# Attention masks of a hybrid decoder block: one mask product of 256 columns per bank instead of one of 128 per diagonal block

## The chip, the core and the metric

The kernel runs on one core of a Trainium2 chip. A core has TensorE for matrix products (PE in the rows, its weight loads PEld), VectorE (DVE), ScalarE (ACT), GpSimd (POOL), and SyncE (SP), which here issues every DMA. The metric is device time in microseconds (us). Before the change it is 869.69 us, the median of three runs from 869.67 to 869.99 us.

## The reference, cut to what matters

The program is one decoder block on 512 tokens of width 1024: RMS norm, a combined input projection, stick-breaking attention and an RWKV-7 branch, a gated merge, a squared-ReLU MLP, a gated embedding and a last norm. The change touches the attention alone, which has 8 heads of 64 channels:

```python
z = jnp.einsum('bhqd,bhkd->bhqk', q[:, :, q0:kend], k[:, :, :kend]).astype(jnp.float32) * scale
mask = s_pos < t_pos
log_om = jnp.where(mask, jax.nn.log_sigmoid(-z), 0.0)
rev = lax.cumsum(log_om, axis=log_om.ndim - 1, reverse=True)
log_w = jax.nn.log_sigmoid(z) + rev - log_om
w = jnp.where(mask, jnp.exp(log_w), 0.0)
```

The mask is strictly causal: a query sees the keys before it. In blocks of 128 keys by 128 queries only the four diagonal blocks need it; blocks under the diagonal are never computed.

## The kernel before, in words

Float32 products are made of pieces in fp32r: a value is split into a high and a low part, and a product of the input projection is three matmuls of 512 columns (lines 191 to 193, high times high, high times low, low times high). Eight such triples make one projected tile of 128 features by 512 tokens, in a PSUM tile `ps_m` or `ps_z`. The split of a loaded weight tile `w_raw` is one ScalarE cast (`w_hi`, line 175) and one VectorE subtraction (`w_lo`, line 176).

Attention works per head, with keys on the partitions and queries along the columns. Of the 4 key blocks j, block j meets the queries from 128 j on, so it has 512, 384, 256 or 128 columns (`ZN`). The scores lie in three PSUM banks: block 2 in one (256 columns), blocks 1 and 3 together in one (384 + 128), block 0 in one (512). `scores` fills the banks in that order. For each block it issues a product with the high part of q (line 458), one with its low part (line 459), and a mask product (line 460): the bf16 identity as weights times `caus_b`, a 128 x 128 tile that holds -1e30 where key >= query and 0 elsewhere, so that the mask is added to the diagonal block in PSUM. That makes 4 masks per head and 32 in all. Per bank follow Abs, Exp and Ln on ScalarE (lines 463 to 465), a VectorE step that gives the softplus `sp` (line 466), and its split into `sph` and `spl` (line 222).

`attend` then adds, into the same banks, the sums over later keys (products with `tri` and `neg`, lines 505 and 509), takes the exponential (ScalarE, line 510), splits it into `wh` and `wl` (VectorE, lines 511 and 512), and multiplies by the values into `ps_o` (line 497). `projected` makes q and k of a pair of heads ready: `qT`, `kT` and `vT` are scaled out of PSUM by VectorE (lines 394, 406, 414), the high parts are cast by ScalarE (400, 409) and GpSimd (401), the low parts `ql` and `kk` come from VectorE (402, 410). Four transposes (line 421) turn the values.

`drive` interleaves the steps of three generators in the source: the attention of one head, the scores of the next, and projection products that fill TensorE's time. The order in which each engine then runs the instructions isn't the order of the source alone: a scheduler places them by its own estimates of their lengths, so a change in a few instructions can move others. Each engine runs its list in order and waits at the first instruction whose operands aren't there.

Of the kernel before, what the change touches and what calls it, by code (L numbers as in the profile page):

```python
# [12 lines left out]
BF16 = mybir.dt.bfloat16  # L13
# [5 lines left out]
P = 128  # L19
# [31 lines left out]
K_ID, K_ONE, K_STRICT, K_INCL, K_B8, K_O8, K_S8, K_BO8, K_BO, K_TRI, K_NEG, K_CAUS = range(12)  # L51
# [34 lines left out]
def tile_block(ctx: ExitStack, tc: tile.TileContext, xT, xt, pT, wts, lora, cols_d, gfin_d, consts_d, out, dbg=None):  # L86
    nc = tc.nc
    act, dve, pool, pe, sync = nc.scalar, nc.vector, nc.gpsimd, nc.tensor, nc.sync
# [3 lines left out]
    def r32(ap):  # L92
        return ap.bitcast(F32)
# [126 lines left out]
    def split(hi, lo, src):  # L220
        act.copy(out=hi, in_=src)  # L221
        dve.tensor_tensor(out=lo, in0=src, in1=r32(hi), op=ALU.subtract)
# [37 lines left out]
    def rstd_of(pool_, ps, ssum, r=None):  # L260

        n = ssum.shape[-1]
        pe.matmul(ps, onesd, ssum, start=True, stop=True)
        if r is None:
            r = pool_.tile([P, T], F32, name="rstd", bufs=2)[:, 0:n]
        nt = pool_.tile([P, T], F32, name="nt", bufs=1)[:, 0:n]
        state["square"] = rsqrt(r, nt, ps)
        return r
# [8 lines left out]
    with ExitStack() as sA:  # L277
# [43 lines left out]
        with ExitStack() as s1:  # L321
            p1 = s1.enter_context(tc.tile_pool(name="p1", bufs=2))
            ps1 = s1.enter_context(tc.tile_pool(name="ps1", bufs=2, space=PSUM))

            def ps_z():
                return ps1.tile([P, T], F32, name="ps_z", bufs=5)

            ZB = [0, 512, 1024, 896]
            ZN = [512, 384, 256, 128]
            BANKS = [(0, 512), (512, 512), (1024, 256)]  # L330

# [44 lines left out]
            first = p1.tile([P, 4 * P], F32, name="first", tag="sums", bufs=1)  # L376
            sync.dma_start(out=first, in_=consts_d[:, NCONST:NCONST + 4 * P])
            tri, neg = (p1.tile([P, P], F32R, name=n, bufs=1) for n in ("tri", "neg"))
            ident_b, caus_b = (p1.tile([P, P], BF16, name=n, bufs=1) for n in ("ident_b", "caus_b"))

            def c1(k):
                return first[:, COFF[k] - NCONST:COFF[k] - NCONST + P]
# [55 lines left out]
            def z(zt, j, lo=0, n=None):  # L438

                b = 0 if j == 0 else (2 if j == 2 else 1)  # L440
                s = ZB[j] - BANKS[b][0] + lo
                n = ZN[j] - lo if n is None else n
                return zt[b][:, s:s + n]

            def scores(hp, hh, got):

                qq, ql, kk = heads[hp][:3]
                sp = p1.tile([P, 1280], F32, name="sp")
                sph = p1.tile([P, 1280], F32R, name="sph")
                spl = p1.tile([P, 1280], F32R, name="spl")  # L450
                zt = {}
                got.update(zt=zt, sp=sp, sph=sph, spl=spl)
                for b, js in BLOCKS:
                    zt[b] = ps_z()

                    for j in js:
                        s = slice(j * P, (j + 1) * P)
                        pe.matmul(z(zt, j), kk[hh][:, s], qq[hh][:, j * P:T], start=j < 3, stop=False, skip_group_check=True)
                        pe.matmul(z(zt, j), kk[hh][:, s], ql[hh][:, j * P:T], start=False, stop=False, skip_group_check=True)
                        pe.matmul(z(zt, j, 0, P), ident_b, caus_b, start=False, stop=True, skip_group_check=True)  # L460
                    s, n = BANKS[b]
                    e = sp[:, s:s + n]
                    act.activation(out=e, in_=zt[b][:, :n], func=AF.Abs)
                    act.activation(out=e, in_=e, func=AF.Exp, scale=-1.0)
                    act.activation(out=e, in_=e, func=AF.Ln, bias=1.0)
                    dve.scalar_tensor_tensor(out=e, in0=zt[b][:, :n], scalar=0.0, in1=e, op0=ALU.max, op1=ALU.add)
                    split(sph[:, s:s + n], spl[:, s:s + n], e)
                    if b == 1:

                        sums = p1.tile([P, 512], F32, name="sums", bufs=1)  # L470
                        hi, lo = (p1.tile([P, 640], F32R, name=name) for name in ("sums_hi", "sums_lo"))
                        for to, i in ((0, 2), (256, 1)):
                            for part, d in ((sph, hi), (spl, lo)):
                                pool.tensor_copy(out=d[:, to:to + P], in_=part[:, ZB[i]:ZB[i] + P])
                        dve.tensor_tensor(out=sums[:, 0:P], in0=sp[:, ZB[2] + P:ZB[2] + 2 * P], in1=sp[:, ZB[3]:ZB[3] + P], op=ALU.add)
                        split(hi[:, P:2 * P], lo[:, P:2 * P], sums[:, 0:P])
                        for c, other in ((0, sp[:, ZB[2]:ZB[2] + P]), (P, sums[:, 0:P])):
                            dve.tensor_tensor(out=sums[:, 256 + c:384 + c], in0=sp[:, ZB[1] + P + c:ZB[1] + 2 * P + c], in1=other, op=ALU.add)
                        pool.tensor_copy(out=hi[:, 384:640], in_=sums[:, 256:512])
                        pool.tensor_tensor(out=lo[:, 384:640], in0=sums[:, 256:512], in1=r32(hi[:, 384:640]), op=ALU.subtract)  # L480
                        got["later"] = hi, lo
                    yield

            def attend(hp, hh, got):
# [8 lines left out]
                def output(js):  # L493

                    for j in js:
                        for part in (wh, wl):
                            pe.matmul(ps_o[:, j * P:T], vv[:, j, hh, :, :].rearrange("p a d -> p (a d)"),  # L497
                                      part[:, ZB[j]:ZB[j] + ZN[j]], start=j == 2 and part is wh, stop=j == 0 and part is wl,
                                      skip_group_check=True)
# [32 lines left out]
            for _ in islice(v, 1):  # L532
# [4 lines left out]
            dve.tensor_copy(out=ident_b, in_=ident)  # L537
            dve.tensor_scalar(out=omm, in0=cols[:, COLS["mu"]:COLS["mu"] + 14], scalar1=-1.0, scalar2=1.0,
                              op0=ALU.mult, op1=ALU.add)
            dve.tensor_copy(out=caus_b, in_=c1(K_CAUS))  # L540
            rstd_of(p1, ps_z(), ssum, rs)
            for i in range(2):
                projected(0, i, pss[i])
# [21 lines left out]
            ahead = with_late(early())  # L565
            NSTEP = 11
            drive((3, scores(*heads_[0], parts[heads_[0]])), (NSTEP, islice(ahead, NSTEP)))
            for n, g in enumerate(heads_):
                todo = [(5, attend(*g, parts[g])), (NSTEP, islice(ahead, NSTEP))]
                if n + 1 < len(heads_):  # L570
                    todo.insert(1, (3, scores(*heads_[n + 1], parts[heads_[n + 1]])))
                drive(*todo)
# [4 lines left out]
        with ExitStack() as s2:  # L577
# [37 lines left out]
            for hp in range(HP):  # L615
                csl = slice(hp * P, (hp + 1) * P)
                for i, (name, got) in enumerate((("w0", cum_), ("a0", a_all))):
# [3 lines left out]
                    t = p2.tile([P, T], F32, name=name, bufs=HP)  # L621
# [497 lines left out]
    def kept(tt):  # L1119
        t = p4.tile([P, 512], F32, name="pl", tag="rk", bufs=4)  # L1120
        return t

    for half in range(2):
        for tt in (half * 2, half * 2 + 1):
            t = kept(tt)
# [222 lines left out]
    with tc.issue_after(s_):  # L1348
        act.preload_act_table_set(LNEXP)

        r, n = (r4[:, i, tt:tt + 1] for i in (1, 2))
# [74 lines left out]
```

## Time and profile before

| what | value |
|---|---|
| median of 3 runs | 869.69 us |
| the profiled execution's own time | 869.75 us |
| its span, first to last instruction | 867.7 us |
| TensorE matmul busy | 851.4 us, 98% of the span |
| VectorE busy | 678.1 us, 78% |
| ScalarE busy | 448.6 us, 52% |
| mask products (line 460) | 32, from 33.0 to 126.9 us |

A row of the timeline gives start, duration, engine, line, operation, and output <- inputs. Matmuls are pipelined: the duration of a short one reaches into those after it, so what a matmul takes from TensorE is read from start to start. A bracket at the end of a row is the idle time before it, and what ended it.

### The profile page before, as it was taken

Reading aid. Unit: us, or ns where it says so; the run is one execution under the profiler, and the core shown is the slowest. Engines: PE = TensorE matmul, PEld = TensorE weight load, DVE = VectorE, ACT = ScalarE, POOL = GpSimd, SP = SyncE. Lnnn points to the kernel's source line nnn. Section 1 sums busy time; section 2 is a strip of 40 time slices with the busy share of each in tenths; the row PEclk is TensorE's granted clock in tenths of the full one; section 3 lists DMA queues with packets and bytes.
Section 4 is the critical chain, followed back from the end, with each engine's and each line's share of the span. In section 5 each row is a group of like instructions: output and inputs, shape, how many; then the busy total and the mean of one; then the engine's idle time right before and its main releaser. Section 6 shows DMA issues by size and latency. Waiting matters only on the chain.

```text
span 867.7 us, 13424 instructions
## 1 busy us (share of the span) xinstructions
PE 851.4 (98%) x5182; PEld 686.8 (79%) x5182; DVE 678.1 (78%) x1228; ACT 448.6 (52%) x703; POOL 80.4 (9%) x138
## 2 busy tenths in 40 slices
PE   8999999999999999999999999999999999999996
PEld 5778787877777777777888888888888888888885
DVE  7899987896979888776754789858985987697767
ACT  6888887744335343534424464344434543453744
POOL 1432431002302111020000000000000000000000
PEclk9999999999999999999999999999999999999999
DMA  7212212221121224437935621531252034300422
GB/s 269 98 49 66 82 62 85 74 97 51 62 87 57 80 73 153 141 116 258 318 121 181 232 73 38 182 120 49 83 184 98 25 127 164 98 1 0 170 73 98
DMA packets 32272, 95.32 MB, mean 110 GB/s; under 512 B 3664, under 2 KB 3664, under 8 KB 32208
## 3 DMA queue, kind: packets, MB, share of 16 engines
q1 hardware_dynamic: 32208, 94.46, 32.6%
q8 instruction: 41, 0.67, 0.3%
q14 instruction: 23, 0.19, 0.1%
HBM read 83.96 MB, written 10.49 MB: 109 GB/s over the span
## 4 chain that ended last, share of the span: by engine, by line
PE 81%; DVE 10%; ACT 4%; issue 1%; DMA 1%; SPq 0%; POOL 0%; POOLq 0%; DVEq 0%; ACTq 0%
PE ps_m L191 13%; PE ps_m L193 13%; PE ps_m L192 13%; PE ps_m L206 9%; PE ps_m L207 9%; PE ps_m L208 9%; DVE w_lo L176 2%; PE ps_g L817 1%; PE ps_o L497 1%; PE ps_g L193 1%; PE ps_c L935 1%; PE ps_s L944 1%; PE ps_g L191 1%; PE ps_g L192 1%; PE ps_g L906 1%
## 5 line engine op out<-in xcount | busy, mean ns | idle before, releaser
L175 ACT CAST w_hi<-w_raw 128x1024 fp32r<-128x1024 f32 x94 | 99.0, 1053 | 170.4 <-PE ps_m L192 110.8
L176 DVE TENSOR_TENSOR w_lo<-w_raw,w_hi 128x1024 fp32r<-128x1024 f32 x94 | 115.1, 1225 | 37.6 <-ACT w_hi L175 37.2
L191 PE MATMUL ps_m<-h_hi,w_hi 128*128 128x512 f32 x320 | 130.6, 410 | 0.9 <-ACT h_hi L353 0.9
L192 PE MATMUL ps_m<-h_lo,w_hi 128*128 128x512 f32 x320 | 128.0, 400 | 0.0
L193 PE MATMUL ps_m<-h_hi,w_lo 128*128 128x512 f32 x320 | 127.5, 399 | 0.0
L191 PE MATMUL ps_m<-hx,w_hi 128*128 128x512 f32 x256 | 99.6, 390 | 0.4 <-ACT hx L1049 0.4
L192 PE MATMUL ps_m<-hx,w_hi 128*128 128x512 f32 x256 | 99.6, 390 | 0.0
L193 PE MATMUL ps_m<-hx,w_lo 128*128 128x512 f32 x256 | 99.5, 389 | 0.0
L191 PEld LDWEIGHTS ps_m<-h_hi,w_hi 128*128 128x128 f32 x320 | 60.7, 190 | 11.4 <-ACT h_hi L353 1.6
L193 PEld LDWEIGHTS ps_m<-h_hi,w_lo 128*128 128x128 f32 x320 | 60.3, 188 | 11.8
L192 PEld LDWEIGHTS ps_m<-h_lo,w_hi 128*128 128x128 f32 x320 | 60.5, 189 | 11.0 <-DVE h_lo L354 1.1
L191 PEld LDWEIGHTS ps_m<-hx,w_hi 128*128 128x128 f32 x256 | 48.0, 188 | 10.5 <-ACT hx L1049 0.6
L192 PEld LDWEIGHTS ps_m<-hx,w_hi 128*128 128x128 f32 x256 | 48.1, 188 | 10.2 <-DVE hx L1050 0.2
L193 PEld LDWEIGHTS ps_m<-hx,w_lo 128*128 128x128 f32 x256 | 48.0, 188 | 10.0
L207 PE MATMUL ps_m<-w_lo,fS 128*128 128x512 f32 x128 | 49.8, 389 | 0.0
L208 PE MATMUL ps_m<-w_hi,fS 128*128 128x512 f32 x128 | 49.8, 389 | 0.0
L206 PE MATMUL ps_m<-w_hi,fS 128*128 128x512 f32 x128 | 49.8, 389 | 0.0
L1291 POOL TENSOR_SCALAR r<-s 128x1 f32<-128x1 f32 x1 | 0.5, 519 | 478.9 <-DVE t L1271 478.9
L208 PE MATMUL ps_m<-w_hi,fA 128*128 128x512 f32 x96 | 37.4, 389 | 0.0
L207 PE MATMUL ps_m<-w_lo,fA 128*128 128x512 f32 x96 | 37.3, 389 | 0.0
L206 PE MATMUL ps_m<-w_hi,fA 128*128 128x512 f32 x96 | 37.3, 389 | 0.0
L221 ACT CAST fS<-sums 128x256 fp32r<-128x256 f32 (+1 forms) x32 | 19.8, 620 | 33.3 <-DVE sums L1141 33.3
(378 smaller groups left out, 1911.6 us busy)
## 6 DMA issues: line engine op xcount, KB each, us to landing
w_raw<-in_wts_dram SPq DMA_DIRECT2D x98, 512.0 KB, 3.5
gates<-gg SPq DMA_DIRECT2D x16, 256.0 KB, 2.1
x_in<-in_xT_dram SPq DMA_DIRECT2D x8, 256.0 KB, 5.7
tmp<-gates SPq DMA_DIRECT2D x8, 256.0 KB, 4.0
upsb<-tmp SPq DMA_DIRECT2D x8, 256.0 KB, 3.5
ga<-upsb SPq DMA_DIRECT2D x8, 256.0 KB, 5.4
gb<-gates SPq DMA_DIRECT2D x8, 256.0 KB, 5.4
xs<-in_xt_dram SPq DMA_DIRECT2D x4, 512.0 KB, 5.9
```

Source lines behind the costliest of these rows:

```text
L175: act.copy(out=hi, in_=raw)
L176: dve.tensor_tensor(out=lo, in0=raw, in1=r32(hi), op=ALU.subtract)
L191: pe.matmul(ps, wh, xh[:, k, t], start=first, stop=False)
L192: pe.matmul(ps, wh, xl[:, k, t], start=False, stop=False)
L193: pe.matmul(ps, wl, xh[:, k, t], start=False, stop=last)
L206: pe.matmul(ps, xh[:, k + j], wh, start=first and j == 0, stop=False, skip_group_check=True)
L207: pe.matmul(ps, xh[:, k + j], wl, start=False, stop=False, skip_group_check=True)
L208: pe.matmul(ps, xl[:, k + j], wh, start=False, stop=last and j == 1, skip_group_check=True)
L221: act.copy(out=hi, in_=src)
L497: pe.matmul(ps_o[:, j * P:T], vv[:, j, hh, :, :].rearrange("p a d -> p (a d)"), part[:, ZB[j]:ZB[j] + ZN[j]], start=j == 2 and part is wh, ...
L817: last = pe.matmul(ps[rows, k], left[rows, k, :], rhs[rows, k], start=True, stop=True)
L906: pe.matmul(ps[:, j * P:(j + 1) * P], Z[:, hh * 4 + g * 2 + cp, :], MA[:, g * 4 + j, :], start=True, stop=True)
```

## The change

Three things change in the attention, and one around it.

1. In the bank of blocks 1 and 3, block 3 now comes first (columns 0 to 127 of the bank) and block 1 behind it (128 to 511), so that both diagonal blocks lie side by side. The table `ZB` says so, and all later steps take their columns from it.
2. `caus_b` grows from one 128 x 128 tile to three side by side: the mask, the mask again, zeros. The zeros are written once by GpSimd, the two masks by one VectorE cast of 256 columns.
3. The mask product moves out of the loop over blocks: one per bank, of 256 columns. For blocks 1 and 3 it takes mask and mask; for a bank with one block it takes mask and zeros. That makes 3 per head and 24 in all, each of 256 columns.
4. The reserved scratch for DMA descriptors written by software shrinks to 2048 bytes per partition, which makes room for the wider tile; every SBUF address moves down by 14,336 or 13,824 bytes.

```diff
-            ZB = [0, 512, 1024, 896]
+            ZB = [0, 640, 1024, 512]
...
-            ident_b, caus_b = (p1.tile([P, P], BF16, name=n, bufs=1) for n in ("ident_b", "caus_b"))
+            ident_b = p1.tile([P, P], BF16, name="ident_b", bufs=1)
+            caus_b = p1.tile([P, 3, P], BF16, name="caus_b", bufs=1)
+            pool.memset(caus_b[:, 2], 0.0)
...
                         pe.matmul(z(zt, j), kk[hh][:, s], ql[hh][:, j * P:T], start=False, stop=False, skip_group_check=True)
-                        pe.matmul(z(zt, j, 0, P), ident_b, caus_b, start=False, stop=True, skip_group_check=True)
+
+                    pe.matmul(z(zt, js[-1], 0, 2 * P), ident_b, caus_b[:, 0:2] if len(js) == 2 else caus_b[:, 1:3], start=False, stop=True,
+                              skip_group_check=True)
...
-            dve.tensor_copy(out=caus_b, in_=c1(K_CAUS))
+            dve.tensor_copy(out=caus_b[:, 0:2], in_=c1(K_CAUS).rearrange("p (o t) -> p o t", o=1).broadcast_to([P, 2, P]))
...
-    nc = bacc.Bacc("TRN2", target_bir_lowering=False, num_devices=1)
+    nc = bacc.Bacc("TRN2", target_bir_lowering=False, num_devices=1, dynamic_dma_scratch_size=2048)
```

From the scores of the fifth of the eight heads on, the lists of all engines are the same as before except for the masks. Up to there the scheduler places other instructions differently too. The line numbers below 376 stay; after it they grow by 2, and after line 460 by 4.

TensorE, first head, bank of blocks 1 and 3 of the scores, before:

```order
L458 MATMUL ps_z<-qq_271,kk_281 128x384
L459 MATMUL ps_z<-ql_193,kk_281 128x384
L460 LDWEIGHTS ident_b
L460 MATMUL ps_z<-caus_b,ident_b 128x128
L458 MATMUL ps_z<-qq_271,kk_281 128x128
L459 MATMUL ps_z<-ql_193,kk_281 128x128
L460 LDWEIGHTS ident_b
L460 MATMUL ps_z<-caus_b,ident_b 128x128
L192 MATMUL ps_m<-h_lo,w_hi 128x512
```

TensorE, the same place after the change, with what now comes behind it:

```order
L460 MATMUL ps_z<-qq_272,kk_282 128x384
L461 MATMUL ps_z<-ql_194,kk_282 128x384
L460 MATMUL ps_z<-qq_272,kk_282 128x128
L461 MATMUL ps_z<-ql_194,kk_282 128x128
L463 LDWEIGHTS ident_b
L463 MATMUL ps_z<-caus_b,ident_b 128x256
L193 MATMUL ps_z<-h_hi,w_lo 128x512
L191 MATMUL ps_z<-h_hi,w_hi 128x512
L192 MATMUL ps_z<-h_lo,w_hi 128x512
L193 MATMUL ps_z<-h_hi,w_lo 128x512
L191 MATMUL ps_m<-h_hi,w_hi 128x512
```

The mask between the two blocks is gone and the one behind them is wider. In this first head the scores also come five projection matmuls earlier: the four of `ps_z` and the first of `ps_m` that stood ahead of them now stand behind. The four transposes, likewise, moved ahead by five matmuls (not shown).

VectorE, the first pair of heads, from `rs` (the norm's factors) on, before and after as one difference:

```order
L257 SCALAR_TENSOR_TENSOR rs<-nt,rs 128x512
-L176 TENSOR_TENSOR w_lo<-w_raw,w_hi 128x1024
-L394 SCALAR_TENSOR_TENSOR qT<-ps_m,rs 128x512
-L406 TENSOR_TENSOR kT<-ps_m,rs 128x512
-L414 TENSOR_TENSOR vT<-ps_z,rs 128x512
+L396 SCALAR_TENSOR_TENSOR qT<-ps_m,rs 128x512
+L408 TENSOR_TENSOR kT<-ps_m,rs 128x512
+L416 TENSOR_TENSOR vT<-ps_z,rs 128x512
```

The weight split `w_lo` that stood ahead of `qT` is gone from here; after the change it stands behind the `kk` of both heads.

VectorE, the third head's attention and the fourth head's first scores, before:

```order
L511 CAST wh<-sp 128x256
L512 TENSOR_TENSOR wl<-sp,wh 128x256
L511 CAST wh<-sp 128x512
L466 SCALAR_TENSOR_TENSOR sp<-ps_z,sp 128x256
L512 TENSOR_TENSOR wl<-sp,wh 128x512
```

VectorE, the same place after the change:

```order
L515 CAST wh<-sp 128x256
L470 SCALAR_TENSOR_TENSOR sp<-ps_z,sp 128x256
L516 TENSOR_TENSOR wl<-sp,wh 128x256
L515 CAST wh<-sp 128x512
L222 TENSOR_TENSOR spl<-sp,sph 128x256
L516 TENSOR_TENSOR wl<-sp,wh 128x512
```

The softplus `sp` of the fourth head's first bank has moved ahead of the third head's `wl`.

## Rows read from the trace of the kernel before

**Rows 1.** The page: the chain that ended last, by engine.
```profile
PE 81%; DVE 10%; ACT 4%; issue 1%; DMA 1%; SPq 0%; POOL 0%; POOLq 0%; DVEq 0%; ACTq 0%
```
**Rows 2.** Windows: stretch, length, PE, PEld, DVE, ACT, POOL busy (instructions), clock, DMA share, GB/s.
```profile
30.00:50.00 20.00, 19.11 (x95) 14.15 (x95) 19.41 (x37) 18.61 (x37) 8.44 (x12) 1.00 0.23 77
50.00:140.00 90.00, 89.11 (x457) 72.90 (x457) 80.65 (x148) 74.02 (x136) 27.17 (x43) 1.00 0.18 62
```
**Rows 3.** Line 460: the mask matmuls, ns min/median/max, first and last start.
```profile
L460 PE MATMUL ps_z<-caus_b,ident_b x32: 229/230/232, 33.0 to 126.9; 128*128 128x128 bf16 x32
```
**Rows 4.** Timeline of PE, bank of blocks 1 and 3: start, us, engine, instruction.
```profile
69.85 0.33 PE L459 MATMUL ps_z<-ql,kk 128*128 128x384 f32 x1
70.03 0.23 PE L460 MATMUL ps_z<-caus_b,ident_b 128*128 128x128 bf16 x1
...
70.32 0.23 PE L460 MATMUL ps_z<-caus_b,ident_b 128*128 128x128 bf16 x1
70.36 0.48 PE L191 MATMUL ps_m<-h_hi,w_hi 128*128 128x512 f32 x1
70.68 0.39 PE L192 MATMUL ps_m<-h_lo,w_hi 128*128 128x512 f32 x1
```
**Rows 5.** Timeline of PE: a matmul of 256 columns and its successors.
```profile
92.74 0.28 PE L509 MATMUL ps_z<-sums_lo,neg 128*128 128x256 f32 x1
92.86 0.40 PE L191 MATMUL ps_m<-h_hi,w_hi 128*128 128x512 f32 x1
93.09 0.40 PE L192 MATMUL ps_m<-h_lo,w_hi 128*128 128x512 f32 x1
```
**Rows 6.** Timeline of DVE: the mask's cast, and the next wait.
```profile
20.74 0.22 DVE L540 CAST caus_b<-first 128x128 bf16<-128x128 f32 x1
...
24.13 1.23 DVE L176 TENSOR_TENSOR w_lo<-w_raw,w_hi 128x1024 fp32r<-128x1024 f32 x1 [2.04 <-ACT w_hi L175]
```
**Rows 7.** Timeline of POOL: its first cast after the memsets.
```profile
29.24 1.28 POOL L401 CAST qq<-qT 64x512 fp32r<-64x512 f32 x2 [25.74 <-DVE qT L394]
```
**Rows 8.** Timeline of PE at the first transposes and the first scores.
```profile
29.69 0.39 PE L191 MATMUL ps_z<-h_hi,w_hi 128*128 128x512 f32 x1
30.43 0.66 PE L421 MATMUL ps_m<-cst,vT 128*128 128x128 f32 x4 [0.35 <-DVE vT L414]
...
32.65 0.36 PE L458 MATMUL ps_z<-qq,kk 128*128 128x256 f32 x1 [0.17 <-DVE kk L410]
```
**Rows 9.** Timeline of DVE from the norm's factors to the low part of k.
```profile
25.99 0.69 DVE L257 SCALAR_TENSOR_TENSOR rs<-nt,rs 128x512 f32<-128x512 f32 x1
27.35 1.23 DVE L176 TENSOR_TENSOR w_lo<-w_raw,w_hi 128x1024 fp32r<-128x1024 f32 x1 [0.67 <-ACT w_hi L175]
28.49 0.68 DVE L394 SCALAR_TENSOR_TENSOR qT<-ps_m,rs 128x512 f32<-128x512 f32 x1
...
31.81 1.41 DVE L410 TENSOR_TENSOR kk<-kT,kk 64x512 fp32r<-64x512 f32 x2
```
**Rows 10.** Timeline of PE in and at the end of the first head's attention.
```profile
38.21 0.47 PE L191 MATMUL ps_m<-h_hi,w_hi 128*128 128x512 f32 x1
38.78 0.33 PE L509 MATMUL ps_z<-sph,neg 128*128 128x128 f32 x1
...
48.60 0.50 PE L497 MATMUL ps_o<-wh,vv 128*128 128x512 f32 x1
...
49.49 0.50 PE L497 MATMUL ps_o<-wl,vv 128*128 128x512 f32 x1 [0.16 <-DVE wl L512]
```
**Rows 11.** Timelines at 68 us: DVE, ACT and PE around the third head's first `wl`.
```profile
68.16 0.42 DVE L512 TENSOR_TENSOR wl<-sp,wh 128x256 fp32r<-128x256 f32 x1
...
68.31 0.41 ACT L465 ACTIVATE sp<-sp 128x256 f32<-128x256 f32 x1
...
68.63 0.39 PE L497 MATMUL ps_o<-wl,vv 128*128 128x256 f32 x1
```
**Rows 12.** Timeline of PE after the long VectorE chain from 82 to 95 us.
```profile
95.63 0.39 PE L497 MATMUL ps_o<-wl,vv 128*128 128x256 f32 x1 [0.55 <-DVE wl L512]
```

## The prediction

> **What bounds the kernel now.** I read the chain of waits first: TensorE carries 81% of it, VectorE 10% [rows 1]. The windows over the attention then show two stretches that differ. From 50 to 140 us TensorE is busy in 89.11 of 90 us; from 30 to 50 us TensorE and VectorE are level, 19.11 and 19.41 of 20 us [rows 2]. So what TensorE no longer does is worth its time after 50 us, and before that only as far as VectorE is earlier too. Third, the starts on TensorE's timeline, since the 0.23 us that a mask is said to last [rows 3] reaches into its successors. From 140 us on nothing is changed in any list, and I let what is won or lost by then pass to the end unchanged.
>
> **What a mask costs.** Behind a mask of 128 columns the next matmul starts 0.04 us later, but that next one then takes 0.32 us to its successor, where the same kind of matmul, not behind a mask, takes 0.23 [rows 4, 5]. A mask therefore costs 0.04 + 0.09 = 0.13 us, though its 128 columns, at the 0.23 us of 512, are worth 0.058. A matmul of 256 columns takes 0.12 us and leaves its successor at the normal 0.23 [rows 5]. I read this as a floor: the next weights need about 0.12 us to load, a matmul of 256 columns covers that and one of 128 doesn't. If so, a mask of 256 columns costs what one of 128 costs.
>
> *The 24 masks that stay, 128 to 256 columns.* By rows 5 the change is 0.12 - 0.13, nothing or a gain of 0.01 each, 0.24 us in all. The other bound is that 128 more columns come on top, 0.058 each, 24 x 0.058 = +1.4 us. I take 0, since a row shows a matmul of that width with just such a successor; that it is fp32r and the mask bf16 is the part that no row shows.
>
> [...]
>
> *The 8 masks that go,* one per head, between the score products of blocks 1 and 3: 8 x 0.13 = 1.0 us of TensorE. If the weight load is left uncovered all the same by the 128-column score product behind it, only the 0.04 is saved, 0.3 us in all. I take 0.13, since the two masks of rows 4 stand in one group of four short matmuls that takes 0.83 us from 69.85 to 70.68, less 0.17 and 0.23 for the long ones at its ends: 0.43 us, or 0.11 per short matmul, whichever kind. Of the eight, two fall before 50 us and are counted below. One, at 82 us, falls into a stretch in which VectorE is the later one: TensorE idles 0.55 us for `wl` at 95.63 [rows 12], at the end of an unbroken run of VectorE work that starts at about 82 us, so that mask only lengthens the idle time. Five remain: 5 x 0.13 = -0.65 us.
>
> **What the moved instructions do at the start.** Before, `rs` is there at 25.99 + 0.69 = 26.7 us, but VectorE first waits 0.67 us for a weight cast and runs `w_lo`, so that `qT` starts at 28.49 [rows 9]. With that `w_lo` moved behind `kk`, `qT` can start at 26.7, `kT` and `vT` behind it. The low parts need ScalarE's casts, and ScalarE is done with its own `w_hi` at about 27.3, so `kk` of the first head moves from 31.81 + 0.7 to about 30.6. The transposes stood at 30.43, though the matmul ahead of them, started at 29.69, leaves TensorE free at 29.92: 0.51 us lost [rows 8]. Five matmuls earlier they would be reached at 29.92 - 5 x 0.23 = 28.8, and `vT` ends at about 28.5: no wait. The first scores are reached 0.41 us (four transposes) and six matmuls (1.4 us) later, at 30.6, when `kk` comes: no wait, or a tenth, where before 0.17 us was idle [rows 8]. So TensorE wins up to 0.7 us here. The moved `w_lo` is for a product that TensorE reaches after 40 us; its weight buffer is refilled some 4 us later, SP's next load being queued for that buffer, and those weights are first cast at about 42 us, so 4 us fit in.
>
> Up to 50 us the total then goes by VectorE, busy in nearly all of it: what it wins is the 0.67 us that it idled ahead of `w_lo`, and a few tenths of later waits. TensorE's waits at 48.60 and 49.49 are for `wh` and `wl` [rows 10]. VectorE now does two more sums of 0.2 us ahead of that `wh`, but TensorE has three more matmuls ahead of that `wl`. I take -0.9 us at 50 us, two masks included. Bounds: -1.6, if all of TensorE's waits that I found in the stretch go: 0.51 and 0.17 from above, 0.25 at 38.78 (0.57 from the start before it, of which 0.32 is a matmul behind a mask), 0.43 from 48.60 to 49.49 (0.89 for two matmuls of 0.23), and two masks, 0.26 [rows 8, 10]; and +0.9 on the other side, worked out with the third rival.
>
> **What they do at 68 us.** `wl` now stands behind the `sp` of the next head's first bank. Before, TensorE started its product with `wl` at 68.63, right behind `wl`'s 68.16 + 0.42 [rows 11]. `sp` needs ScalarE's Ln (line 465), which ended at 68.31 + 0.41; its list changed too, so that the Ln comes ahead of a 512-column exponential and ends at about 68.3. Then `sp` takes 0.34, `wl` follows from 68.65 on and ends near 69.07: TensorE waits 0.47 us more. Behind `wl` stand two `wh` and a split, which TensorE needs only at 72 us. Bounds: 0, if VectorE is ahead of TensorE by then, and 0.5. I take +0.47.
>
> **What is hidden.** The cast of `caus_b` grows from 0.22 us by at most that much and stands ahead of a VectorE wait of 2.04 us [rows 6]; GpSimd's memset lies in a wait of 25.74 us [rows 7]. Without that cover they would cost 0.22 us and the length of a small memset. The smaller scratch changes addresses only; no DMA here is issued by GpSimd.
>
> **The sum.** -0.65 - 0.9 + 0.47 = -1.08 us, on the profiled execution's 869.75 (867.7 of span and 2.05 around it), which is 0.06 above the median: 868.7, or 868.6 against the median. Its own range is 867.6 to 869.4.
>
> **Rivals.**
> First, more is won at the start: all these waits go, -1.6, the one at 68 us doesn't come, and the five masks give -0.65: -2.25, or 867.5 (between 866.8 and 867.9). For it: nearly all of them are for VectorE, whose list lost an idle stretch. Against it: VectorE is busy 97% of that stretch, so it can hardly be 1.6 us earlier.
>
> Second, a mask costs by its columns: 24 x 0.115 - 32 x 0.058 = +0.9 us, of which about 0.8 lies where TensorE is the later one. With the start without its masks (-0.64) and +0.47: +0.6, or 870.3. For it: bf16 and fp32r needn't behave alike. Against it: 0.13 us per mask in the trace before, more than twice its columns. [...]
>
> Third, the other side: the early scores stop TensorE. They stand five projection matmuls earlier in its list, and if `kk` isn't earlier (the point is 31.5 us: `kk` later than that costs more than the waits that go), TensorE stands still with five matmuls behind them, 5 x 0.23 = 1.16 us, that were done by then before. +1.16 - 0.26 - 0.65 + 0.47 = +0.7, or 870.4; with the columns' price on top 871.3. For it: VectorE's `kk` waits on ScalarE, which is as busy. Against it: the 1.8 us between `rs` and `qT` that are freed [rows 9].
>
> **Chances.** 0.62 for the forecast, 0.22 for the first rival, 0.08 each for the second and third. A difference under 0.2%, 1.74 us, can't be told from none by a measurement of this kernel. Faster by more means below 867.95: the first rival and the low end of the forecast, 0.27. Slower by more means above 871.4, the two last rivals at their upper ends and beyond: 0.07. Within: 0.66. The range of 866.8 to 870.9 leaves out the low end of the first rival and the upper ends of the others.
>
> **What would show it.** In the profile of the changed kernel: 24 masks; from mask start to the second start behind it some 0.36 us, as before, and not 0.42; the first transposes with no idle time ahead of them at about 28.8 us and the first scores at about 30.7; the product at 49.49 about 0.9 us earlier; a wait of some 0.5 us for `wl` near 68 us; a longer one near 95 us; and all work from 140 us on shifted by one amount. The prediction is wrong if masks lengthen their banks, if TensorE idles over 1 us ahead of the first scores, or if a stretch behind 140 us changes its length.

## The result, and the profile after

The changed kernel takes 873.75 us (median of 6 runs, 872.39 to 874.27) against 869.70 (868.96 to 869.99): 1.0047 times as long, interval 1.0036 to 1.0058. Forecast were 868.6 us and a range of 866.8 to 870.9: sign and range are both missed. Medians here and below are over all executions; a ratio needn't agree to the last digit with the quotient of the medians beside it. The profiled execution took 873.83 us, 872.0 of them span; before it was 869.75 and 867.7.

The chain of waits of the kernel after, by engine; it answers to [rows 1]:
```profile
PE 79%; DVE 11%; ACT 6%; DMA 2%; issue 2%; SPq 0%; POOL 0%; POOLq 0%; ACTq 0%; DVEq 0%
```
"issue", time in which an engine waits for nothing that the profile shows, has grown from 1% to 2%. The windows say where. This is the kernel after, columns as in [rows 2], whose two stretches come first:
```profile
30.00:50.00 20.00, 17.99 (x89) 13.62 (x88) 19.45 (x34) 17.07 (x34) 7.44 (x12) 1.00 0.25 79
50.00:140.00 90.00, 88.69 (x452) 72.99 (x451) 80.43 (x147) 73.88 (x136) 27.51 (x43) 1.00 0.18 62
...
300.00:301.00 1.00, 0.10 (x7) 0.00 (x0) 0.44 (x1) 0.52 (x1) 0.00 (x0) 1.00 0.00 0
301.00:302.00 1.00, 0.00 (x0) 0.00 (x0) 0.24 (x1) 0.00 (x0) 0.00 (x0) 1.00 0.00 0
302.00:303.00 1.00, 0.94 (x19) 0.79 (x20) 0.44 (x2) 0.01 (x1) 0.00 (x0) 1.00 0.00 0
303.00:304.00 1.00, 1.00 (x4) 0.45 (x2) 1.00 (x4) 1.00 (x1) 0.00 (x0) 0.67 0.07 16
304.00:306.00 2.00, 2.00 (x67) 1.67 (x67) 1.20 (x3) 0.64 (x2) 0.00 (x0) 0.50 0.31 123
```
From 30 to 50 us TensorE is busy 1.1 us less than before at the same VectorE time. Near 300 us, some 170 us behind the last mask (127.2 us), it stands still for two microseconds, and right after that its granted clock reads 0.67 and then 0.50, where it read 1.00.

TensorE's timeline after, at the places that the prediction named and at 300 us (start, length, instruction, idle time ahead of it and who ended that):
```profile
28.47 0.60 PE L423 MATMUL ps_m<-cst,vT 128*128 128x128 f32 x4
...
30.59 0.36 PE L460 MATMUL ps_z<-qq,kk 128*128 128x256 f32 x1
...
31.55 0.28 PE L463 MATMUL ps_z<-caus_b,ident_b 128*128 128x256 bf16 x1
31.59 0.47 PE L193 MATMUL ps_z<-h_hi,w_lo 128*128 128x512 f32 x1
31.91 0.39 PE L191 MATMUL ps_z<-h_hi,w_hi 128*128 128x512 f32 x1
...
38.45 0.33 PE L513 MATMUL ps_z<-sph,neg 128*128 128x128 f32 x1 [0.36 <-ACT sph L221]
...
39.96 0.33 PE L513 MATMUL ps_z<-spl,neg 128*128 128x128 f32 x1 [0.66 <-DVE spl L222]
...
49.37 0.50 PE L501 MATMUL ps_o<-wh,vv 128*128 128x512 f32 x1 [0.86 <-DVE wh L515]
...
50.86 0.50 PE L501 MATMUL ps_o<-wl,vv 128*128 128x512 f32 x1
...
69.79 0.38 PE L501 MATMUL ps_o<-wl,vv 128*128 128x256 f32 x1 [0.60 <-DVE wl L516]
...
96.17 0.39 PE L501 MATMUL ps_o<-wl,vv 128*128 128x256 f32 x1 [0.55 <-DVE wl L516]
...
299.24 0.87 PE L821 MATMUL ps_g<-LX,LB 32*32 32x64 f32 x47
302.06 0.46 PE L821 MATMUL ps_g<-LX,LB 32*32 32x64 f32 x17 [1.96 <-issue]
302.46 0.50 PE L192 MATMUL ps_m<-h_lo,w_hi 128*128 128x512 f32 x1
```
The same run of 64 small products in the kernel before is unbroken:
```profile
298.91 1.10 PE L817 MATMUL ps_g<-LX,LB 32*32 32x64 f32 x64
299.94 0.50 PE L192 MATMUL ps_m<-h_lo,w_hi 128*128 128x512 f32 x1
```
Subtracting the start of each TensorE instruction before from its start after gives the account. TensorE is 0.3 us ahead at 28.1 us, and 0.94 ahead at 33.8 (after: 32.83). It is 0.68 behind at 50.5, 1.16 behind at 70, and 0.30 behind from 123 to 299 us. The stop takes that to 2.52 behind (299.94 to 302.46), the low clock to 3.55 at 303.2 of before, and some 3.4 stay. Behind 838 us ScalarE and VectorE lose 0.8 more, while TensorE stays at 3.4: a weight load landed late, and the last cast of weights waits 3.49 us for it in ScalarE's timeline after,
```profile
838.60 1.05 ACT L175 CAST wg<-w_raw 128x1024 fp32r<-128x1024 f32 x1 [3.49 <-DMA w_raw<-in_wts_dram]
```
and 2.08 before. So 0.3 + 2.2 + 1.0 + 0.8 = 4.3 us of span. No run aimed at the late load. Experiments 1 and 6 below wait 2.18 and 1.93 us at this cast, so I take it for scatter of this execution.

### The profile page after: what moved, and what is told of

Its sections match the earlier page's. It is cut to its first block, busy times and chain, and to the rows that moved or that the text cites. A ratio compares the mean times of both kernels' runs of the same rounds, so it can differ in the third digit from the quotient of the medians.

```text
span 872.0 us, 13404 instructions
## 1 busy us (share of the span) xinstructions
PE 851.7 (98%) x5174; PEld 687.8 (79%) x5174; DVE 679.3 (78%) x1228; ACT 449.7 (52%) x703; POOL 80.5 (9%) x139
## 4 chain that ended last, share of the span: by engine, by line
PE 79%; DVE 11%; ACT 6%; DMA 2%; issue 2%; SPq 0%; POOL 0%; POOLq 0%; ACTq 0%; DVEq 0%
PE ps_m L191 14%; PE ps_m L193 14%; PE ps_m L192 14%; PE ps_m L207 7%; PE ps_m L208 7%; PE ps_m L206 7%; DVE w_lo L176 1%; ACT hx L1053 1%; PE ps_o L501 1%; DMA w_raw<-in_wts_dram 1%; PE ps_g L821 1%; PE ps_g L193 1%; PE ps_g L192 1%; PE ps_g L191 1%; PE ps_g L910 1%
```

## What stopped TensorE: the theory

The page of the kernel after counts the packets on the queues by which instructions are fetched:
```profile
q8 instruction: 41, 0.67, 0.3%
```
That is 41 packets of 16 KB; 5174 matmuls and as many weight loads make 10,348 instructions, 252 for each packet, so I take this queue to bring TensorE's list, in blocks of some 252 instructions. The same line, asked of single stretches of one microsecond: before, a block moves between 294 and 295 us and none from 295 to 300,
```profile
q8 instruction: 1, 0.02, 8.9%
```
after, none between 294 and 295, and one between 299 and 300:
```profile
q8 instruction: 1, 0.02, 5.8%
```
That lies within a dense part: from 297.14 on (after: 297.47) TensorE issues 160 small products and their weight loads, 320 instructions, more than a block, before in 2.8 us. Eight masks fewer are 16 instructions fewer. My theory, the block theory: every block's boundary then lies 16 instructions later in the work; in the kernel before, TensorE comes to the point where the next block is asked for just before the work that it has to wait for at 297 us; after the change, just behind it. The block's packet starts at 294.57 before, 2.57 us ahead of the dense part, and at 299.73 after, 2.26 us behind the start of it. TensorE goes on at 302.06, 2.33 us behind the packet's start; by the theory it had used up what it had.

Rivals: the tiles' other addresses (smaller scratch), and the new order of the start.

## Experiments on the stop

Each ratio is against runs of the kernel before on the same chip, beside it.

**1. Sixteen instructions put back at the start.**
```
             for _ in range(12):
                 pe.matmul(ps, warm[:, 0:P], warm, start=True, stop=True)
+            for _ in range(8):
+                pe.matmul(ps[:, 0:32], warm[:, 0:P], warm[:, 0:32], start=True, stop=True)
```


> The changed kernel with eight more products of 32 columns behind the twelve warming ones: 16 instructions more in TensorE's list, which then has as many as before the change; the order of all other work is the same. Block theory: the 1.96 us stop at 300 us comes from a 16 KB block of TensorE's instructions that is asked for too late, because the list is 16 instructions shorter; the stop and the half clock behind it go, 3.1 us less, 870.6 us (869.9 to 870.9). Rival (addresses of tiles, or the new order of the start): the stop stays, 873.7 us (873.3 to 874.2).

869.85 us, 1.0007 (0.9998 to 1.0015): 3.9 us less than the changed kernel, for eight useless products more, and a little under the expected range. TensorE's timeline has no gap at 300 us, but a smaller one, in another run of small products, at 356:
```profile
299.45 1.10 PE L823 MATMUL ps_g<-LX,LB 32*32 32x64 f32 x64
...
356.80 0.37 PE L823 MATMUL ps_g<-LX,LB 32*32 32x32 f32 x18 [0.74 <-issue]
```

**2. Sixteen instructions taken out of the kernel before**, eight warming products.
```
-            for _ in range(12):
+            for _ in range(4):
```

> The kernel before with four warming products in place of twelve: 16 instructions fewer in TensorE's list, as after the change; no mask, tile or other instruction is changed. Block theory: a stop of about 2 us in the run of small products near 300 us and a half clock behind it, 869.7 + 3.1 = 872.8 us (872.0 to 873.5). Rival (addresses or order): no stop, 869.7 us (869.3 to 870.2), plus at most 0.5 us at the start if the clock rises later.

873.02 us, 1.0036 (1.0024 to 1.0048). That a clock which rises later costs up to 0.5 us at the start was my estimate; the windows don't show it, the clock reads 1.00 in all of them from 0 to 28 us. The stop is there, in a kernel without any of the change, at the same count of products (47 and 17):
```profile
298.07 0.86 PE L817 MATMUL ps_g<-LX,LB 32*32 32x64 f32 x47
300.94 0.46 PE L817 MATMUL ps_g<-LX,LB 32*32 32x64 f32 x17 [2.00 <-issue]
```
One of its windows behind the stop; the clock, the third number from the end, reads 1.00, as it does from 299 to 301:
```profile
304.00:306.00 2.00, 2.00 (x39) 1.53 (x38) 1.96 (x5) 0.73 (x2) 0.00 (x0) 1.00 0.34 131
```
and this execution took 871.96 us; the changed kernel's, with the half clock, took 873.83. Of the five profiled executions that stop at 300 us, three show the half clock behind it (the changed kernel, with 0.50; experiments 6 and 7, where the first product of 512 columns behind the stop lasts 0.80 and 0.79 us) and two don't (this one and 5, where it lasts 0.50). The kernel before, which doesn't stop, reads 1.00 from 299 to 304. The low clock thus follows the stop in some executions and not in others.

**3. The kernel before with the smaller scratch alone.**
```
-    nc = bacc.Bacc("TRN2", target_bir_lowering=False, num_devices=1)
+    nc = bacc.Bacc("TRN2", target_bir_lowering=False, num_devices=1, dynamic_dma_scratch_size=2048)
```

> The kernel before with the smaller scratch area of the change alone; tiles lie at other addresses. Block theory: 869.7 us (869.4 to 870.0), no stop. Address theory: the stop at 300 us, 872 to 874 us.

869.57 us, 0.9997 (0.9988 to 1.0006), no stop. The addresses are out.

**4. The change with 32 separate masks of 128 columns.**
```
-                    pe.matmul(z(zt, js[-1], 0, 2 * P), ident_b, ..., start=False, stop=True, ...)
+                        pe.matmul(z(zt, j, 0, P), ident_b, caus_b[:, 0], start=False, stop=True, ...)
```


> The changed kernel with one mask product of 128 columns for each block again (32, not 24): the new places of the blocks, the wider mask tile and nearly the new order of the start stay, TensorE's list is as long as before. Block theory: no stop at 300 us; 870.6 (the changed kernel without the stop) + 5 effective masks of 0.13 us = 871.2 us (870.6 to 871.6), TensorE at 50 us 0.7 to 1.0 us later than before the change. Order theory: the stop stays, 874.4 us (873.8 to 875).

870.01 us, 0.9998 (0.9989 to 1.0007), no stop, as the block theory had it, but 1.2 us less than expected. What I expected at 50 us was wrong: TensorE is 0.55 us *ahead* of before there, not behind. With 32 masks the other engines' lists are not quite those of the change; the next section is on that.

**5. Separate masks in the last four heads alone** (28 masks, 8 instructions short of before).
```
+                        if 2*hp+hh >= 4:
+                            pe.matmul(z(zt, j, 0, P), ident_b, caus_b[:, 0], start=False, stop=True, ...)
+                    if not (2*hp+hh >= 4):
                         pe.matmul(z(zt, js[-1], 0, 2 * P), ident_b, ..., start=False, stop=True, ...)
```

> The changed kernel with separate masks in the last four heads: 28 mask products, order of the change, TensorE's list 8 instructions longer than after the change and 8 shorter than before. Block theory: all or nothing. Either the stop of 2 us stands at 300 us, 873.75 + 0.4 = 874.2 us (871.5 to 874.8), or it is gone, 869.85 + 0.4 = 870.3 us (869.8 to 870.7). The four masks show as 0.13 us each on TensorE between 70 and 125 us, 0.4 to 0.5 us together. A theory in which the stop grows with the number of instructions gives about half of the loss, 872.1 us with a stop of 1 us.

873.21 us, 1.0035 (1.0021 to 1.0048), with the stop:
```profile
302.07 0.53 PE L823 MATMUL ps_g<-LX,LB 32*32 32x64 f32 x21 [1.67 <-issue]
```
It stands 4 products earlier, 8 instructions, as the theory has it of the boundary, and has not halved: all or nothing, as expected. The four masks cost 0.31 us between 60 and 130 us; I had expected 0.4 to 0.5, and a part is again lost in the wait at 95 us.

**6. and 7. Two controls on the changed kernel:** the eight small products near 400 us, behind the stop; and a thirteenth warming product of 512 columns, meant to give the delay of the first experiment with 2 instructions in place of 16 (`range(12)` becomes `range(13)`).
```
+                if len(done) == HP - 1:
+                    for _ in range(8):
+                        pe.matmul(ps[0:32, 0:32], ident[0:32, 0:32], ident[0:32, 0:32], start=True, stop=True)
```


> The changed kernel with eight products of 32 columns near 400 us, behind the place of the stop: TensorE's list is as long as before, but nothing moves in it up to 300 us. Block theory: the stop of 2 us stays, 873.75 + 0.1 = 873.8 us (872.4 to 874.4). Rival (the length of the whole list decides): no stop, 869.9 us.

> The changed kernel with a thirteenth warming product of 512 columns: the start is delayed by 0.4 us, as by eight small products, but the list grows by 2 instructions, not 16. Block theory: the stop stays, 873.75 + 0.3 = 874.0 us (872.4 to 874.7). Rival (the delay at the start cured it): no stop, 869.9 us.

874.93 us, 1.0060 (1.0048 to 1.0072), and 872.55 us, 1.0037 (1.0025 to 1.0048). The stop, first behind the late padding,
```profile
302.39 0.69 PE L821 MATMUL ps_g<-LX,LB 32*32 32x64 f32 x17 [1.86 <-issue]
```
then behind the longer warming, with 18 products left, for two instructions more in the list:
```profile
301.99 0.52 PE L821 MATMUL ps_g<-LX,LB 32*32 32x64 f32 x18 [1.83 <-issue]
```
The first is 0.5 us over its expected range (TensorE is 0.43 later than in the changed kernel already at 297 us, and stops again, for 0.48 us, at 359.94); the second lies in its own. The second did not delay the start (first real product at 5.96 us, 6.05 before), so it tests the boundary alone. What a delay does is seen from where TensorE stands at 297 us: it stops when 0.84 us ahead of before (experiment 2) and when 0.76 behind (6), and doesn't when 0.55 ahead (4), 0.54 behind (1) or 2.08 behind (14, below). So in these runs neither the length of the list as a whole nor a delay decides; that it is where the boundary lies in the work is the reading left.

The traces of all eighteen kernels, the later experiments too, agree. In the five that stop here 1980, 1981 or 1984 products stand ahead of the dense part; in the other thirteen 1988 or 2004. In the five the block's packet starts 1.85 to 2.31 us behind the start of the dense part, in the thirteen 2.15 to 2.96 us ahead of it. And in each of the five TensorE goes on 2.2 to 2.5 us behind the start of that packet. From this I infer that TensorE waits for this block, and that the block comes late because its transfer starts late; why it starts late, and at which instruction it is asked for, is not shown: no view has the request.

**8. and 9. More padding:** `range(8)` of experiment 1 becomes `range(24)`; and 22 such products on the kernel of experiment 10 in place of its six.

> The changed kernel with 24 small products at the start, 48 instructions more than after the change and 32 more than before; order of the change. Block theory: no stop at 300 us nor at 356 us, 869.85 + 0.2 for the products at the start - 0.4 for the stop at 356 us, 869.6 us (869.2 to 870.0). Rival: the small products themselves helped (the clock at the start), and more of them move the time further, under 869.2 or over 870.2 us.

> As the run before, with 16 more small products at the start: 32 instructions more in TensorE's list, all of its blocks asked for earlier in the runs of small products. Block theory: no stop at 300 us, and that of 0.75 us at 356 us, which some executions show, goes too: 868.9 us (868.4 to 869.3), with less scatter. Rival (the stop at 356 us has another cause): as the run before, 869.3 us.

872.24 us, 1.0025 (1.0016 to 1.0035), and 870.68 us, 1.0006 (0.9997 to 1.0014). Both expectations were wrong. No stop at 300 us, but others, which I put down to other boundaries in other dense runs; the kernel with 24 products:
```profile
251.26 0.50 PE L192 MATMUL ps_m<-h_lo,w_hi 128*128 128x512 f32 x1 [0.44 <-issue]
...
357.54 0.50 PE L823 MATMUL ps_g<-LX,LB 32*32 32x32 f32 x34 [0.76 <-issue]
```
That with 22 stops 0.57 us at 249.91. Padding was no margin here: both lengths brought stops elsewhere. (With the 24 products TensorE is also about a microsecond later at 33.8 us than in the changed kernel.)

## Experiments on the order and the masks

Between 33.8 and 50.5 us of before TensorE loses 1.62 us in the changed kernel (from 0.94 ahead to 0.68 behind), and 1.61 to 1.63 in each run with its order (experiments 1, 5, 6, 7, 8, 12, 16). With the order of experiment 4 it loses 0.50 to 0.54 (4, 9, 10, 11, 14, 15). That order comes back when only the first and the fourth head keep separate masks, but for two projection products of TensorE's own list.

**10. 26 masks, list as long as before.** Experiment 5 with another condition, and six small products as in experiment 1.
```
+                        if 2*hp+hh in (0, 3):
```

> The changed kernel with separate masks in the first and the fourth head alone (26 mask products) and six small products at the start, so that TensorE's list is as long as before; the other engines then have word for word the order of the run with 32 masks, not that of the change. Order theory: TensorE is 0.5 us or more ahead of before at 50 us where the change was 0.7 behind, and the six masks left out show as 0.13 us each later: 1.2 us ahead at 290 us, 870.0 - 0.7 = 869.3 us (868.7 to 869.5). Rival (the loss at 40 to 70 us is that of the mask of 256 columns itself or of the earlier scores): behind at 50 us as after the change, 869.85 us (869.6 to 870.2).

869.46 us, 0.9998 (0.9988 to 1.0009). The stretch costs 0.53 us, not 1.62. I had put a start 0.4 us later down to the small products (first real product at 6.44 us in experiment 1, with eight of them, against 6.05), but the runs don't show that: it comes at 5.94 here, with six, and at 5.87 to 6.34 in experiments 3 to 7, with none. 11 and 12, made for that reason, trade one warming product for small ones:

**11. 26 masks and 12. the whole change, with one warming product less** (11: 7 small products; 12: 9, and no condition).
```
-            for _ in range(12):
+            for _ in range(11):
                 pe.matmul(ps, warm[:, 0:P], warm, start=True, stop=True)
+            for _ in range(7):
+                pe.matmul(ps[:, 0:32], warm[:, 0:P], warm[:, 0:32], start=True, stop=True)
```

> 26 masks in the order of the run with 32, with eleven warming and seven small products: list as long as before and no delay at the start. TensorE 0.3 us ahead of before at 290 us, no stop at 300 us: 869.6 - 0.3 = 869.3 us (868.8 to 869.6). Rival (masks and order move nothing that reaches the end): 869.6 us, as before.

> The change whole, with eleven warming and nine small products: list as long as before and no delay at the start. Order theory: TensorE 0.6 us less its lead at the start behind before at 290 us, 869.6 + 0.5 = 870.1 us (869.6 to 870.5), above the run with 26 masks by 0.5 to 0.9. Rival: the order costs nothing, 869.0 us.

869.07 us, 0.9996 (0.9987 to 1.0004), and 870.55 us, 1.0012 (1.0003 to 1.0021). Ten of the eleven times of the first lie from 868.69 to 869.55 (the eleventh, the profiled 870.78, has a stop of 1.14 us at 356 us), all of the second from 870.11 to 871.30: 1.5 us between two kernels of one length of list (0.5 to 0.9 were expected), the one with two masks *fewer* being the slower. At 297 us their TensorE timelines stand 0.3 ahead of and 0.78 behind before. The whole change without its stop is therefore still about 0.9 us slower than before, and the 26 masks, half a microsecond faster in the median, can't be told from before: nothing here clearly beats both kernels.

One place where the order loses is VectorE's list ahead of the products at 49 us; the change:
```profile
48.28 0.29 DVE L479 TENSOR_TENSOR sums<-sp 128x128 f32<-128x128 f32 x1
48.49 0.29 DVE L482 TENSOR_TENSOR sums<-sp 128x128 f32<-128x128 f32 x1
48.69 0.28 DVE L482 TENSOR_TENSOR sums<-sp,sums 128x128 f32<-128x128 f32 x1
48.89 0.42 DVE L515 CAST wh<-sp 128x512 fp32r<-128x512 f32 x1
49.23 0.88 DVE L222 TENSOR_TENSOR spl<-sp,sph 128x512 fp32r<-128x512 f32 x1
50.03 0.77 DVE L516 TENSOR_TENSOR wl<-sp,wh 128x512 fp32r<-128x512 f32 x1
```
and the 26 masks:
```profile
47.47 0.40 DVE L483 TENSOR_TENSOR sums<-sp 128x128 f32<-128x128 f32 x1
47.80 0.68 DVE L222 TENSOR_TENSOR spl<-sp,sph 128x512 fp32r<-128x512 f32 x1
48.40 0.41 DVE L519 CAST wh<-sp 128x512 fp32r<-128x512 f32 x1
...
49.03 0.68 DVE L520 TENSOR_TENSOR wl<-sp,wh 128x512 fp32r<-128x512 f32 x1
49.63 0.28 DVE L486 TENSOR_TENSOR sums<-sp 128x128 f32<-128x128 f32 x1
49.84 0.28 DVE L486 TENSOR_TENSOR sums<-sp,sums 128x128 f32<-128x128 f32 x1
```
In the change two further sums stand ahead of `wh`, and the split `spl` between `wh` and `wl`; in the other the split stands ahead of both and the sums behind. `wl` comes 1.0 us later, and TensorE starts its product at 50.86. But the first rows of the two lists are already 0.81 us apart (48.28 and 47.47), so that the order shown here is 0.2 of the 1.0. The largest single difference lies earlier: at 39.96 the change waits 0.66 us for `spl`, where the 26 masks wait 0.10 (39.61). How the 1.1 us divide over the moved instructions, TensorE's own among them, no run takes apart. At 68 us the 26 masks show no wait for `wl` at all, the change 0.60.

**13. to 16. A leaner start** (lists as long as before): the kernel before, then the change with 32, 26 and 24 masks, with 8, 8, 14 and 16 small products.
```
-            for _ in range(12):
+            for _ in range(4):
                 pe.matmul(ps, warm[:, 0:P], warm, start=True, stop=True)
+            for _ in range(8):
+                pe.matmul(ps[:, 0:32], warm[:, 0:P], warm[:, 0:32], start=True, stop=True)
```

> The kernel before with four warming products and eight products of 32 columns in place of twelve warming ones: TensorE's list as long as before, order as before. Block theory: no stop at 300 us, where the run with four warming products and a shorter list had one of 2.00 us; TensorE is as far ahead there as in that run, 0.8 us, so 869.6 - 0.8 = 868.8 us (868.4 to 869.3). Rival (the fewer warming products brought that stop, not the length of the list): a stop, 872 to 873 us.

> The same start, with the new places of the blocks and the wider mask tile, but 32 separate masks; list as long as before. The new order of the start does not wait for the transposes, so the leaner warming gives it less: 870.0 - 0.3 = 869.7 us (869.0 to 869.9). Nothing of the loss at 40 to 70 us (order theory); rival: that loss belongs to the places of the blocks, and TensorE is behind before at 50 us.

> As the run before, with 26 masks (separate ones in the first and the fourth head), the same order on the other engines and the same length of TensorE's list. Mask theory: six times 0.13 us, 0.7 to 0.8 us less than the run before: 868.9 us (868.3 to 869.1), and TensorE 0.7 us or more ahead of that run at 130 us. Rival (removed products are given back at the next wait): same as the run before.

> The change whole (24 masks, its own order) with the same start and length of list. Order theory: TensorE loses at 38 to 70 us what it had gained, as in the changed kernel, and ends behind the run with 26 masks though it has two masks fewer: 869.3 us (869.0 to 869.8). Rival (order costs nothing): two masks less than the run with 26, 868.7 us.

870.19, 871.29, 870.50 and 870.63 us; ratios 1.0008, 1.0012, 1.0008 and 1.0011, each with some 0.001 to either side; all four expectations were missed. The base failed: TensorE was 1.49, 1.83 and 0.83 us late and 0.51 early at 28.1 us. In the second of the four it got through 11 matmuls from 10 to 14 us,
```profile
10.00:14.00 4.00, 4.00 (x11) 3.14 (x11) 4.00 (x7) 4.00 (x9) 0.00 (x0) 1.00 0.63 206
```
where the same line of the kernel before counts 18 and that of the fourth 20. So the times tell nothing of masks. One thing the traces do tell: with four warming products and a list as long as before (13) there is no stop at 300 us, so experiment 2's came from the list.

## Why the prediction was wrong

**The step that failed most:** "From 140 us on nothing is changed in any list, and I let what is won or lost by then pass to the end unchanged." The lists' content was unchanged, but, by the block theory, not their place in the blocks in which they are fetched. This cost the 1.96 us stop, the low clock behind it (together 3.2 us of TensorE's account above), and 3.9 us in the median by experiment 1. No rival had it. Why the block's transfer starts late stays open.

**The second step that failed is the start: -0.9 us at 50 us.** It measured +0.68. Without the stop, too, the change would have lost: 0.9 us by experiment 12, where 1.08 were to be won. The first half came as worked out: transposes at 28.47 without a wait (forecast 28.8), scores at 30.59 (30.6), 0.94 ahead at 33.8 us. Then it was lost. I wrote that VectorE's win was the 0.67 us it had idled; at `wh`, 48.89 against 48.12 before, it was 0.77 behind. And TensorE's waits, which I let go, grew: 0.36 us at 38.45, 0.66 at 39.96 and 0.86 at 49.37, where there had been 0.10, none and 0.11 (idle time in front of the same products). Part of VectorE's loss is seen in its rows after,
```profile
34.03 1.67 DVE L176 TENSOR_TENSOR w_lo<-w_raw,w_hi 128x1024 fp32r<-128x1024 f32 x1
...
36.05 1.09 DVE L404 TENSOR_TENSOR ql<-qT,qq 64x512 fp32r<-64x512 f32 x1
...
37.78 0.69 DVE L404 TENSOR_TENSOR ql<-qT,qq 64x512 fp32r<-64x512 f32 x1
```
the first two some 0.4 us longer than elsewhere (1.23 in [rows 9], 0.69 in the last row), and part in its order at 48 us, where the kernel before had
```profile
47.91 0.29 DVE L475 TENSOR_TENSOR sums<-sp 128x128 f32<-128x128 f32 x1
48.12 0.42 DVE L511 CAST wh<-sp 128x512 fp32r<-128x512 f32 x1
48.46 0.28 DVE L478 TENSOR_TENSOR sums<-sp 128x128 f32<-128x128 f32 x1
48.66 0.78 DVE L512 TENSOR_TENSOR wl<-sp,wh 128x512 fp32r<-128x512 f32 x1
49.36 0.68 DVE L222 TENSOR_TENSOR spl<-sp,sph 128x512 fp32r<-128x512 f32 x1
```
From the first sum to `wh` it took 0.21 us before and 0.61 after. I saw these two sums and let them be paid by three matmuls moved ahead of `wl`'s product; but those stand behind `wh`'s product, and it is `wh` that TensorE waits for. They do cover the split `spl` that now stands between `wh` and `wl` (0.80 us), which I didn't name. I weighed counts of instructions and not their times. The forecast's bound of +0.9 for this term did hold it.

**The masks: right.** A mask of 256 columns costs 31.91 - 31.55 = 0.36 us to the second start behind it, as forecast, not 0.42. Each removed one shows as 0.12 to 0.14 us later (from 0.68 behind to 0.55 at 57 us, 1.16 to 1.04 at 70, 0.54 to 0.41 at 97): the price of 0.13 holds, and the price by columns (second rival) falls. That the weight load, which I estimated at 0.12 us from [rows 5], is the floor behind this price is a reading that no run tests.

**The wait at 68 us: right in kind.** +0.57 (from 0.59 behind to 1.16) against +0.47.

**The wait at 95 us: right in kind, opposite in sign.** VectorE's unbroken run does set the time there; but TensorE came later than before, not earlier, and got 0.36 us back (from 0.90 behind at 94.0 us to 0.54).

## What to carry over

Here sixteen instructions fewer in TensorE's list were enough: a run of 320 short instructions that took 2.8 us stood still before its end for 1.96 us (2.00 in experiment 2), some 170 us behind the last mask and in unchanged code; with sixteen put back (experiment 1) it didn't. So look, in the profile before, for such runs and for the instruction packets near them; and if a small edit costs some microseconds at a place that it doesn't touch, put the same number of instructions back ahead of that place before judging the edit. And where a scheduler orders all engines' work, what a removed product is worth can be less than what the new order costs: here 0.3 us, for six masks (TensorE gains 0.29 from 28 to 130 us in experiment 11, and 0.01 in experiment 4 with all 32), against 1.1.

## Not expected of the hardware

- TensorE stood still for 0.44 to 2.00 us, with no releaser in the profile, at three places (250, 300 and 356 to 360 us). There are fourteen such stops in the eighteen profiled executions, and at each TensorE goes on 2.2 to 2.8 us behind the start of a block's packet. At 356 us the place in the list alone doesn't decide: with one length of list ahead of it, experiments 1, 10, 11 and 15 stop there, and the kernel before, 3, 4, 12, 13, 14 and 16 don't.
- The half clock behind the long stop came in three of five profiled executions. Among the times of kernels without that stop are some of over 872 us at a mean clock of 0.993 to 0.996 (one each in experiments 1 and 13, two in 10); they have no trace, and what happened there is open.
- VectorE and GpSimd at the same time: in the change GpSimd's `qq` cast started at 34.02 and took 0.61 us, VectorE's `w_lo` at 34.03 took 1.67. In experiment 4 VectorE was first (33.74, 1.22 us) and the same cast, from 33.78, took 1.65. In both, the instruction that started second was the long one; why is not shown, and no run here tries it alone.
- With four warming products in place of twelve TensorE stood at 28 us anywhere from 0.51 us early to 1.83 late (experiments 2 and 13 to 16), though the granted clock reads 1.00 in all windows from 0 to 28 us (experiments 2, 13, 14 and 16). The cause is open.
